# Hybrid decoder block on one core: the opening's hand-written order carried on to the fourth product of the first seven-product block

## The chip, the core and the metric

One core of a Trainium2 chip runs the whole program: TensorE (PE in the profile) multiplies, VectorE (DVE) and ScalarE (ACT) prepare operands and post-process, GpSimd (POOL) fills a few constants, SyncE (SP) issues the large transfers. PEld are TensorE's weight loads. The metric is the device time of one execution in microseconds (us). The kernel before takes 1735.16 us, the median of 3 runs (1734.92 to 1735.41).

## What is computed

A macaron block: a SwiGLU feed-forward part, a token mixer, a second feed-forward part, and a norm. The change touches the start of the first feed-forward part, and the place where the mixer's small vectors are loaded.

```python
D_MODEL, SEQ, D_FF, FFN_RESIDUAL_SCALE = 2048, 256, 5632, 0.5

def rms_norm(x, gain):
    var = jnp.mean(x * x, axis=-1, keepdims=True)
    return x * lax.rsqrt(var + NORM_EPS) * gain

def swiglu_ffn(x, w_gate, w_up, w_down):
    return (jax.nn.silu(x @ w_gate) * (x @ w_up)) @ w_down

x = x + FFN_RESIDUAL_SCALE * swiglu_ffn(rms_norm(x, ffn1_norm), w_gate, w_up, w_down)
...
z = rms_norm(x, mix_norm) @ w_in
```

Everything is float32. x has 256 rows of 2048 columns, the gate and up matrices have 2048 x 5632 elements.

## The kernel before

**Products in three parts.** A float32 operand is split into a high part (a cast to a shorter format, called `hi`, made by ScalarE) and a low part (`lo`, the rest, made by VectorE as a difference). A product is then hi x hi, lo x hi and hi x lo, accumulated in one bank of the accumulator memory. Weights come in units of 512 rows by 512 columns: four slices of 128 rows. One unit of weights against one half of x (128 rows) is 12 matrix instructions of 128x512: 8 with the weights' high part, 4 with their low part; against both halves it is 24 (`multiply`, lines 211 to 226). A unit is loaded as `raw`, 1 MB. `parts_of` (line 197) makes `hi` in two casts of 128x1024 and `lo` in one instruction of 128x2048. High and low parts live in two rotating buffers and, for every third unit, in a third one (`split_tiles`, line 183), so a new unit's cast waits until the product that used its buffer is done.

**The first 512 columns of gate and up** are made by `begin` (line 569), whose order is written out by hand and kept on every engine, since `Engine.pinned` is set (lines 36 to 44, 671). x has four parts of 512 columns, called units 0 to 3. Units 0 and 1 are transposed unnormalised (`turn`, with the gain applied), since the norm's factor is only known when all of x has been squared; the banks are scaled by the factor afterwards (`scale_banks`). Units 2 and 3 are normalised first and then transposed (`scaled`, `turn_scaled`). `squares` sums the squares on ScalarE, `factor` and `diagonals` make the factor, `rows` spreads it by two small products. `plain` keeps the sum of the transposed high and low parts for units 0 and 1, which `scale` and `split` later turn into normalised operands. Before the data arrive, `keep_busy` issues dummy products on a bank that nobody reads; they keep TensorE working.

**The seven-product blocks.** All further columns of gate and up go through `seven` (line 377) in pairs of 512 columns. For units 0 and 1 of x and two columns of weights it is a two-by-two block product with seven products instead of eight, with sums of weights (`w12 - w11`, `w22 - w11`, `w22 - w12`, `w21 - w11`, on VectorE, in place) and sums of x (`seven_of`: `spare`, `two`, `last`, with `high` and `low` for their split). Units 2 and 3 of x take part as ordinary products (`usual`). TensorE's work in the block, in program order:

- `product_of(0)`, `product_of(4)`: 12 instructions each; in the profile `ps_g_a` and `ps_g_c`, with weights `hi_g_p`, `lo_g_p`
- `usual(0, b2)`: 24, into `ps_g_e` and `ps_g_c`, with `hi_g_x`, `lo_g_x`
- `product_of(5)`: 12; `usual(1, b3)`: 24; `product_of(6)`: 12; `product_of(2)`: 12
- `usual(0, a2)`: 24; `product_of(3)`: 12; `usual(1, a3)`: 24; `product_of(1)`: 12

The results `a` and `c` of some products are copied out by ScalarE (`snap`: `s1`, `s5`, `u2`, `u3`), since the bank is used again or the value is needed twice. `between` is called at fixed places with a number or a name and lets the caller put other work there. In the kernel before, `meanwhile` (line 773) drops the pinning at the first of these places, after the second product; from there a list scheduler orders every engine's work but SyncE's, by its own model of the times. After the third product it makes the remaining sums of x (`sums`), after the fourth the hidden tiles of the first 512 columns (`first_hidden`: silu of gate times up).

**Queues.** The large loads are issued by SyncE in the order of the program. GpSimd issues ten small loads of vectors for the mixer at the very start (`load_vectors`, lines 116 and 138 to 161): two groups, `many` and `conv`, which `prepare` (line 801) transposes much later, in the middle of the first feed-forward part.

In `begin` the loop over the four slices of unit 0 stands like this:

```python
for j in range(UK):
    norm.turn((j,))
    high(0, "g", quarters[j : j + 1])
    low(0, "g", quarters[j : j + 1])
    if j:
        products(j - 1)
products(UK - 1)
```

Of the kernel before, what the change touches and what calls it, by code (L numbers as in the profile page):

```python
# [49 lines left out]
def hybrid_block(ctx: ExitStack, tc: tile.TileContext, a: dict, out: bass.AP):  # L50
# [53 lines left out]
    act.activation(early, ones[:, :1], AF.Copy, scale=1.0)  # L104
# [11 lines left out]
    def load_vectors(group, name, engine):  # L116
# [19 lines left out]
    keep_busy(2)  # L136
    pe.held = False
    turns = [
        load_vectors(
            [  # L140
                ("mix_norm", a["mix_norm"][0], 16),
                ("ffn2_norm", a["ffn2_norm"][0], 16),
                ("lru_lambda", a["lru_lambda"][0], 8),
                ("lru_conv_b", a["lru_conv_b"][0], 8),
                ("lru_b_a", a["lru_b_a"][0].rearrange("h d -> (h d)"), 8),
                ("lru_b_i", a["lru_b_i"][0].rearrange("h d -> (h d)"), 8),
                ("lru_out_norm", a["lru_out_norm"][0], 8),
                ("sc_out_norm", a["sc_out_norm"][0], 8),
            ],
            "many",  # L150
            nc.gpsimd,
        ),
        load_vectors(
            [
                ("lru_conv_w", a["lru_conv_w"][0].rearrange("k d -> (k d)"), 32),
                ("sc_conv_w", a["sc_conv_w"][0].rearrange("k d -> (k d)"), 24),
            ],
            "conv",
            nc.gpsimd,
        ),  # L160
    ]
# [49 lines left out]
    def multiply(targets, blk, apart=False, middle=None, late=None):  # L211
# [4 lines left out]
        for ps, st, begin, _ in targets:  # L216
            for j in range(UK):
                pe.matmul(ps, st[j][0], blk[j][0], start=begin and j == 0, stop=False, **more)
                pe.matmul(ps, st[j][1], blk[j][0], start=False, stop=False, **more)
# [9 lines left out]
    class Norm:  # L229
# [5 lines left out]
        def squares(self, c):  # L235
            for t in range(NT):
# [109 lines left out]
    def seven_of(sf, x0, x1, v, spare, parts):  # L346
# [25 lines left out]
        high(4)  # L372
        low(4)
# [5 lines left out]
    def seven(w, rows, cols, sf, xs, name, keep, done, between=None):  # L379
# [23 lines left out]
        def usual(i, raw, n, *targets):  # L403

            blk = parts_of(raw, f"{name}_x{i}{n}")
# [36 lines left out]
    def ffn(tag, norm, after, opening=False):  # L442
        with tc.tile_pool(name=f"ffn{tag}", bufs=1, side="left") as fp:
# [89 lines left out]
            def sums():  # L533

                if not left:
                    pair = [big(f"xs{tag}_{i}") for i in range(2)]
                    halves = [(b[:, :, o : o + P], b[:, :, o + P : o + S]) for b in pair for o in (0, S)]
                    left.append(seven_of(sf, units[0], units[1], vs, quad(keep(f"spare{tag}")), halves))
# [26 lines left out]
            def joint(u, m, blk, middle=None, late=None):  # L565
                x = norm.xT[u] if u < 2 else units[u]
                multiply([(ps[m, t], stationary(x, t), u == 0, u % 2 == 1) for t in range(NT)], blk, True, middle, late)

            def begin():
# [17 lines left out]
                def mm(u, m, middle=None, late=None):  # L587
                    joint(u, m, blocks(*parts[u, m]), middle, late)
# [14 lines left out]
                for j in range(UK):  # L603
# [38 lines left out]
                mm(1, "u", norm.rows, lambda: turn_both(2))  # L642
# [21 lines left out]
                sums()  # L664
                low(3, "u")
# [17 lines left out]
            def first_hidden():  # L683
                for t in range(NT):
# [3 lines left out]
                    waiting.append((0, t, sg, False))  # L688

# [60 lines left out]
            for s in range(5):  # L750
# [22 lines left out]
                def meanwhile(i):  # L773
                    if i == "sum":
                        return
# [359 lines left out]
```

## Time and profile before

| | us |
|---|---|
| median of 3 runs | 1735.16 |
| the profiled execution, its own time | 1735.13 |
| its span, from the first to the last instruction | 1733.4 |
| TensorE busy in the span | 1722.0 |
| VectorE busy | 1478.2 |
| ScalarE busy | 1047.3 |
| GpSimd busy | 6.9 |

The granted TensorE clock over the span is 0.999 of full speed. A row of the timeline has the start, the duration, the engine, the line, the operation, what it writes and reads with shapes, and the number of instructions merged into it; in brackets how long the engine stood idle before, and what it waited for. Nearly all instructions carry line 43, that of the wrapper `Engine`, so the tile names tell them apart: `ps` are accumulator banks, `pt` and `ph` transposes, `raw` loaded weights, `xres` is x, `xT` and `x` its transposed operands, `xs` the operands made of sums, `junk` the squares. A trailing letter or number of a buffer is left out of the names.

In rows by stretches of time, each engine's busy time and number of instructions are followed by the granted clock, the busy share of the transfer engines, and the GB/s they moved.

### The profile page before, as it was taken

How to read it: one execution, taken by the hardware profiler on the slowest of the kernel's cores; microseconds unless marked ns; L12 is line 12 of the kernel's file. 1: busy time of each engine (PE TensorE's matmuls, PEld its weight loads, DVE VectorE, ACT ScalarE, POOL GpSimd, SP SyncE). 2: the span in 40 equal slices, each digit the busy share in tenths (PEclk: the TensorE clock that was granted, in tenths of full speed). 3: DMA queues.
4: the chain of work that ended last, by engine and by line, in shares of the span. 5: the costliest groups of instructions: out<-in, count | busy, mean ns of one | idle time of the engine just before them, and what ended most of it. 6: DMA issues, size and time to landing. Idle time of an engine off the chain costs nothing.

```text
span 1733.4 us, 20352 instructions
## 1 busy us (share of the span) xinstructions
PE 1722.0 (99%) x8045; PEld 1439.9 (83%) x8045; DVE 1478.2 (85%) x1213; ACT 1047.3 (60%) x1354; POOL 6.9 (0%) x32
## 2 busy tenths in 40 slices
PE   9999999999999999999999999999999999999998
PEld 8788888888888888888888888888888888888886
DVE  7998989889789898687986668889899888899895
ACT  7666565656466666565655446656556664556654
POOL 1000000000000000000000000000000000000000
PEclk9999999999999999999999999999999999999999
DMA  7664665566466556555555764565665646555743
GB/s 275 213 219 146 217 221 192 199 238 218 151 205 210 201 180 218 172 170 193 177 189 183 247 209 137 194 243 177 215 214 194 215 149 218 194 194 195 255 157 122
DMA packets 174224, 343.24 MB, mean 198 GB/s; under 512 B 5684, under 2 KB 8624, under 8 KB 174000
## 3 DMA queue, kind: packets, MB, share of 16 engines
q1 hardware_dynamic: 173632, 340.81, 57.5%
q8 instruction: 63, 1.03, 0.2%
q10 hardware_dynamic: 176, 1.06, 0.2%
q14 instruction: 33, 0.27, 0.0%
q0 software_dynamic: 320, 0.07, 0.0%
HBM read 339.82 MB, written 2.10 MB: 197 GB/s over the span
## 4 chain that ended last, share of the span: by engine, by line
PE 97%; DVE 2%; issue 0%; DMA 0%; ACT 0%; DVEq 0%
PE ps_d L43 13%; PE ps_in L43 13%; PE ps_u_a L43 9%; PE ps_g_a L43 9%; PE ps_u_c L43 6%; PE ps_g_c L43 6%; PE ps_d_a L43 5%; PE ps_o L43 5%; PE ps_u_d L43 5%; PE ps_g_d L43 5%; PE ps_d_c L43 3%; PE ps_u_e L43 3%; PE ps_g_e L43 3%; PE ps_g L43 3%; PE ps_u L43 3%; PE ps_d_d L43 3%
## 5 line engine op out<-in xcount | busy, mean ns | idle before, releaser
L43 ACT CAST hi_g_p<-raw_g 128x1024 fp32r<-128x1024 f32 x140 | 142.5, 1050 | 103.1 <-DVE raw_g L43 28.3
L43 DVE TENSOR_TENSOR lo_g_p<-raw_g,hi_g_p 128x2048 fp32r<-128x2048 f32 x70 | 159.5, 2287 | 33.3 <-ACT hi_g_p L43 33.1
L43 ACT CAST hi_u_p<-raw_u 128x1024 fp32r<-128x1024 f32 x140 | 141.3, 1049 | 68.4 <-PE ps_u_a L43 22.9
L43 DVE TENSOR_TENSOR lo_u_p<-raw_u,hi_u_p 128x2048 fp32r<-128x2048 f32 x70 | 159.2, 2287 | 20.6 <-ACT hi_u_p L43 20.2
L43 PE MATMUL ps_d<-hi_d,h 128*128 128x512 f32 x704 | 168.0, 390 | 0.0
L43 PEld LDWEIGHTS ps_d<-hi_d,h 128*128 128x128 f32 x704 | 131.5, 188 | 26.9
L43 PE MATMUL ps_in<-xT_nm,hi_in 128*128 128x512 f32 x640 | 153.4, 391 | 0.1
L43 PEld LDWEIGHTS ps_in<-xT_nm,hi_in 128*128 128x128 f32 x640 | 117.4, 188 | 23.5 <-DVE bc_nm L43 0.6
L43 ACT CAST hi_d<-raw_d 128x1024 fp32r<-128x1024 f32 x88 | 88.6, 1047 | 70.0 <-PE ps_u_d L43 22.4
L43 DVE TENSOR_TENSOR lo_d<-raw_d,hi_d 128x2048 fp32r<-128x2048 f32 x44 | 100.6, 2290 | 30.5 <-ACT hi_d L43 30.5
L43 DVE TENSOR_TENSOR lo_in<-raw_in,hi_in 128x2048 fp32r<-128x2048 f32 x40 | 91.4, 2286 | 39.4 <-ACT hi_in L43 35.5
L43 ACT CAST hi_in<-raw_in 128x1024 fp32r<-128x1024 f32 x80 | 80.0, 1045 | 67.2 <-PE ps_in L43 46.0
L43 ACT CAST hi_d_p<-raw_d 128x1024 fp32r<-128x1024 f32 x84 | 85.0, 1049 | 58.8 <-DVE raw_d L43 40.0
L43 ACT CAST hi_g_x<-raw_g 128x1024 fp32r<-128x1024 f32 x80 | 81.4, 1048 | 42.2 <-PE ps_g_c L43 24.6
L43 ACT CAST hi_u_x<-raw_u 128x1024 fp32r<-128x1024 f32 x80 | 80.5, 1047 | 36.5 <-PE ps_u_c L43 19.6
L43 DVE TENSOR_TENSOR lo_d_p<-raw_d,hi_d_p 128x2048 fp32r<-128x2048 f32 x42 | 95.6, 2287 | 7.8 <-ACT hi_d_p L43 7.7
L43 DVE TENSOR_TENSOR raw_u<-raw_u,raw_u 128x2048 f32<-128x2048 f32 x40 | 91.6, 2290 | 9.3 <-DMA raw_u<-in_ffn_w_up_dram 8.6
L43 DVE TENSOR_TENSOR lo_g_x<-raw_g,hi_g_x 128x2048 fp32r<-128x2048 f32 x40 | 91.5, 2286 | 6.6 <-ACT hi_g_x L43 6.6
L43 DVE TENSOR_TENSOR raw_g<-raw_g,raw_g 128x2048 f32<-128x2048 f32 x40 | 91.5, 2289 | 3.4 <-DMA raw_g<-in_ffn_w_gate_dram 2.9
L43 DVE TENSOR_TENSOR lo_u_x<-raw_u,hi_u_x 128x2048 fp32r<-128x2048 f32 x40 | 91.4, 2286 | 2.1 <-ACT hi_u_x L43 1.9
L43 PE MATMUL ps_d<-lo_d,h 128*128 128x512 f32 x352 | 87.3, 389 | 0.0
L43 PEld LDWEIGHTS ps_in<-xT_nm,lo_in 128*128 128x128 f32 x640 | 82.1, 191 | 3.1
(363 smaller groups left out, 3568.7 us busy)
## 6 DMA issues: line engine op xcount, KB each, us to landing
raw_d<-in_ffn_w_down_dram SPq DMA_DIRECT2D x88, 1024.0 KB, 5.1
raw_u<-in_ffn_w_up_dram SPq DMA_DIRECT2D x87, 1024.0 KB, 5.1
raw_g<-in_ffn_w_gate_dram SPq DMA_DIRECT2D x86, 1024.0 KB, 5.1
raw_in<-in_w_in_dram SPq DMA_DIRECT2D x40, 1024.0 KB, 5.0
raw_o<-in_w_out_dram SPq DMA_DIRECT2D x16, 1024.0 KB, 5.1
xres<-in_x_dram SPq DMA_DIRECT2D x3, 512.0 KB, 10.2
raw_g<-in_ffn_w_gate_dram SPq DMA_DIRECT2D x4, 256.0 KB, 5.1
raw_u<-in_ffn_w_up_dram SPq DMA_DIRECT2D x2, 512.0 KB, 8.7
```

The lines of the kernel that those rows point to most:

```text
L43: ins = getattr(self.engine, name)(*args, **kwargs)
```

## The change

1. The first activation, which loads ScalarE's function table, is a square root instead of a copy, so the table with the square root is loaded at the start and not at the norm's factor.
2. The two dummy products between the transposition of the first gain vector and the first transposes of x are gone. One is issued ahead of the first products instead, and the last two slices of unit 0 are transposed before the second slice's products.
3. The transfers of the second half of up's unit 0 and of gate's unit 1 are issued earlier than x's second and third quarters, respectively.
4. Squares, casts and low parts from unit 0 of up to unit 1 of up are cut into halves and interleaved in another order. `multiply` takes `pieces`: the products with high parts go over both halves of x for the first two slices, then for the last two. `within` places the transposes of unit 1 inside up's unit 0.
5. `low(3, "u")` stands between the cast and the low part of the first sum of x.
6. In the first block of gate (`early`) the pinning holds until the fourth product of sums is done (`product_of(6)`). The sums of x are made at named places: `two` after `w12 - w11`; the casts and low parts of two operands behind the second product; `last` with its cast and low part after `w22 - w12`. `w22 - w11` and the parts of `b2` are made earlier, with one cast of 128x2048. `first_hidden` follows the copy `u3`.
7. The mixer's vectors are loaded after `first_hidden`: `load_vectors` first copies a column of the second hidden tile into the row tile on GpSimd, so its loads wait for that tile.

The core of the diff:

```diff
-    act.activation(early, ones[:, :1], AF.Copy, scale=1.0)
+    act.activation(early, ones[:, :1], AF.Sqrt)
...
-    def load_vectors(group, name, engine):
+    def load_vectors(group, name, engine, after=None):
...
+        if after is not None:
+            engine.tensor_copy(rows[:, :1], after[:n, :1])
...
     first_turn()
-    keep_busy(2)
     pe.held = False
-    turns = [
-        load_vectors(
...
+    turns = []
+    def load_more(after):
+        turns.extend(
...
-    def multiply(targets, blk, apart=False, middle=None, late=None):
+    def multiply(targets, blk, apart=False, middle=None, late=None, pieces=(range(UK),), within=None):
...
+        for js in pieces:
+            for i, (ps, st, begin, _) in enumerate(targets):
+                if within and js is pieces[-1] and i == len(targets) - 1:
+                    within()
+                for j in js:
...
         dve.tensor_tensor(spare, a21, a22, op=ALU.add)
         high(4)
+        if meanwhile:
+            meanwhile()
         low(4)
...
         product_of(0, w11, a, True)
         dve.tensor_tensor(w11, w12, w11, op=ALU.subtract)
+        if early:
+            between("first sum")
         product_of(4, w11, c, True)
-        s1 = snap(a, "s1")
+        blk = None
+        if early:
+            between("second product")
+            hi, lo = split_tiles(f"{name}_x01")
+            act.copy(hi, b2)
+            s1 = snap(a, "s1")
+            dve.tensor_tensor(w11, w22, w11, op=ALU.subtract)
+            low_part(b2, hi, lo)
+            blk = blocks(hi, lo)
+        else:
+            s1 = snap(a, "s1")
         s5 = snap(c, "s5")
...
-        usual(0, b2, 1, (e, 1, True, not two), (c, 0, False, False))
+        usual(0, b2, 1, (e, 1, True, not two), (c, 0, False, False), first=blk)
...
-        dve.tensor_tensor(w11, w22, w11, op=ALU.subtract)
+        if not early:
+            dve.tensor_tensor(w11, w22, w11, op=ALU.subtract)
...
         dve.tensor_tensor(w12, w22, w12, op=ALU.subtract)
+        if early:
+            between("third sum")
         product_of(6, w12, a)
         u3 = snap(a, "u3")
+        if early:
+            between("fifth product")
...
-                    if j:
-                        products(j - 1)
-                products(UK - 1)
-
-                fetch(0, "u", ends, lambda i: load_x(1) if i == 0 else None)
+                    if j == 1:
+                        keep_busy(1)
+                        products(0)
+                for j in range(1, UK):
+                    products(j)
+
+                fetch(0, "u", ends)
+                load_x(1)
+                fetch(1, "g", ends)
                 load_x(2)
-                fetch(1, "g", ends)
                 load_x(3)
-                high(0, "u")
-                his, los = turn(1)
-                his()
-                norm.squares(0)
-                low(0, "u", ends)
-                los()
+                js = (range(2), range(2, UK))
+                high(0, "u", ends[:1])
+                norm.squares(0, (0,))
+                low(0, "u", ends[:1])
+                high(0, "u", ends[1:])
+                norm.squares(0, (1,))
+                low(0, "u", ends[1:])
+
+                def second():
+                    his, los = turn(1)
+                    his()
+                    los()
+
+                mm(0, "u", None, None, js, second)
+
+                high(1, "g")
                 plain(0)
-                mm(0, "u")
-
-                high(1, "g")
+                low(1, "g", ends)
+                plain(1)
                 norm.squares(1)
                 norm.squares(2)
-                low(1, "g", ends)
-                plain(1)
-                mm(1, "g")
+                mm(1, "g", None, None, js)
 
                 fetch(1, "u")
                 fetch(2, "g")
-                high(1, "u")
-                norm.squares(3)
-                low(1, "u")
+                norm.squares(3, (0,))
+                high(1, "u", ends[:1])
+                norm.squares(3, (1,))
+                low(1, "u", ends[:1])
+                high(1, "u", ends[1:])
                 norm.factor()
                 norm.diagonals()
+                low(1, "u", ends[1:])
...
-                sums()
-                low(3, "u")
+                sums(lambda: low(3, "u"))
...
+                if opening:
+                    load_more(sg)
...
                     if opening and s == 0:
-                        Engine.pinned = False
-                        if i:
-                            (sums, first_hidden)[i - 1]()
+                        two, last, high, low = left[0]
+                        if i == "first sum":
+                            two()
+                        elif i == "second product":
+                            for k in (5, 6):
+                                high(k)
+                                low(k)
+                        elif i == "third sum":
+                            last()
+                            high(2)
+                            low(2)
+                        elif i == "fifth product":
+                            Engine.pinned = False
+                            first_hidden()
...
-                seven(wg, (0, 1), cs, sf, xs, f"g{tag}_{s}", keep, gate, meanwhile)
+                seven(wg, (0, 1), cs, sf, xs, f"g{tag}_{s}", keep, gate, meanwhile, opening and s == 0)
```

More of the change, by code (lines that the diff above doesn't have):

```diff
@@ L209, in stationary @@
         return [(tile[:, j, t * P : (t + 1) * P], tile[:, j, S + t * P : S + (t + 1) * P]) for j in range(UK)]
-    def multiply(targets, blk, apart=False, middle=None, late=None):
+    def multiply(targets, blk, apart=False, middle=None, late=None, pieces=(range(UK),), within=None):
         more = dict(skip_group_check=True) if apart else {}
[L216 to L219, printed above, removed]
+        for js in pieces:
[3 more added lines that the diff above has]
+                for j in js:
+                    pe.matmul(ps, st[j][0], blk[j][0], start=begin and j == 0, stop=False, **more)
+                    pe.matmul(ps, st[j][1], blk[j][0], start=False, stop=False, **more)
         if middle:
@@ L233, in __init__, with squares @@
             self.ss = work.tile([P, NT, NC_D], F32, tag="ss", name=f"ss_{name}")
-        def squares(self, c):
-            for t in range(NT):
+        def squares(self, c, ts=range(NT)):
+            for t in ts:
                 junk = work.tile([P, CW], F32, tag="junk", name=f"junk_{self.name}_{c}_{t}", bufs=1)
@@ L341, in product, with seven_of @@
         return ps
-    def seven_of(sf, x0, x1, v, spare, parts):
+    def seven_of(sf, x0, x1, v, spare, parts, meanwhile=None):
         a11, a12, a21, a22 = v[0, 0], v[0, 1], v[1, 0], v[1, 1]
@@ L377, in quad, with seven @@
         return tile.rearrange("p (j c) -> p j c", j=UK)
-    def seven(w, rows, cols, sf, xs, name, keep, done, between=None):
+    def seven(w, rows, cols, sf, xs, name, keep, done, between=None, early=False):
         a, c, e, d = (bank(f"ps_{name}_{n}") for n in "aced")
@@ L531, in normalise, with sums @@
                 split(u)
-            def sums():
+            def sums(meanwhile=None):
                 if not left:
@@ L537, in sums @@
                     halves = [(b[:, :, o : o + P], b[:, :, o + P : o + S]) for b in pair for o in (0, S)]
-                    left.append(seven_of(sf, units[0], units[1], vs, quad(keep(f"spare{tag}")), halves))
+                    spare = quad(keep(f"spare{tag}"))
+                    left.append(seven_of(sf, units[0], units[1], vs, spare, halves, meanwhile))
                 else:
@@ L585, in low, with mm @@
                         low_part(*(z[:, i:e, :] for z in [raw[u, m]] + parts[u, m]))
-                def mm(u, m, middle=None, late=None):
-                    joint(u, m, blocks(*parts[u, m]), middle, late)
+                def mm(u, m, *more):
+                    joint(u, m, blocks(*parts[u, m]), *more)
                 def turn(c):
```

59 lines of the change are left out of this document (31 added, 28 removed).

## The prediction, made before the changed kernel was run

> **What bounds the kernel now.** I read the page's totals and its chain first, then the list of waits, then the chain in order of time.
>
> ```profile
> span 1733.4 us, 20352 instructions
> PE 1722.0 (99%) x8045; PEld 1439.9 (83%) x8045; DVE 1478.2 (85%) x1213; ACT 1047.3 (60%) x1354; POOL 6.9 (0%) x32
> ...
> PE 97%; DVE 2%; issue 0%; DMA 0%; ACT 0%; DVEq 0%
> ```
>
> TensorE is busy for 99% of the span and makes 97% of the chain that ended last. Only where it stands still, or runs slowly, is there anything to win. The list of its waits, over the whole run, has three entries:
>
> ```profile
> PE idle L43 <- DVE ones L43: 1.1, 1, 1.1
> PE ps_g_e L43 <- DVE lo_g_x L43: 0.8, 1, 0.8
> PE ps_g L43 <- ACT hi_g L43: 0.6, 1, 0.6
> ```
>
> All three lie in the part that the diff rewrites. The chain in order of time shows how much is lost there (start, duration, work, number of instructions):
>
> ```profile
> 3.83 1.15 PE idle L43 x4
> 4.98 0.44 PE pt_n L43 x2
> ...
> 5.44 0.47 ACT xT_n L43
> 5.92 0.52 ACT hi_g L43
> ...
> 6.48 2.93 PE ps_g L43 x6
> ...
> 9.82 1.38 PE ps_g L43 x6
> ...
> 14.20 0.87 PE pt_n L43 x8
> ...
> 49.98 5.45 PE ps_u L43 x24
> ...
> 97.52 2.72 PE ps_u_a L43 x12
> ```
>
> 24 products in 5.45 us are 0.227 us each; eight transposes in 0.87 us are 0.109 each. From the first transpose (4.98) to 14.20 stand 24 products and 8 transposes, 6.3 us of work in 9.22: 2.9 lost. From 14.20 to the first product of the block (49.98 + 5.45 = 55.43) nearly nothing is lost. The block's 180 products (15 groups of 12) need 40.9 us and take 97.52 - 55.43 = 42.1: 1.2 lost. With the 4.98 before the first transpose, that is about 9 us; nothing else can be won here. The sum is made against this execution's 1735.13 us (span 1733.4 and 1.7 around it), 0.03 below the median of the runs.
>
> **The opening.** Two dummy products stand ahead of the first transposes: the filler runs to 4.98, and the transposes follow at once. Had their data landed by then? Issue to landing, four transfers issued at 0.74, 1.23, 2.20 and 2.68:
>
> ```profile
> xres<-in_x_dram SPq DMA_DIRECT2D x1, 256.0 KB, 3.2
> raw_g<-in_ffn_w_gate_dram SPq DMA_DIRECT2D x1, 256.0 KB, 3.3
> xres<-in_x_dram SPq DMA_DIRECT2D x1, 256.0 KB, 6.4
> raw_g<-in_ffn_w_gate_dram SPq DMA_DIRECT2D x1, 256.0 KB, 6.5
> ```
>
> The first x piece is there at 3.94, so without that filler the transposes start near 4.05, 0.93 earlier. The copy of the transposed x (0.47) and the cast of the weights (0.52; landed at 4.53) follow them, so the first product starts at about 5.55 instead of 6.48. The one dummy that is left, now ahead of it, runs in the gap of that wait (two passes of 1.15/4 = 0.29 us, to about 5.5) and costs nothing.
>
> Those first products are slow:
>
> ```profile
> 6.48 2.08 PE L43 MATMUL ps_g<-hi_g,xT_n 128*128 128x512 f32 x4 [0.64 <-ACT hi_g L43]
> 9.48 1.27 PE L43 MATMUL ps_g<-hi_g,xT_n 128*128 128x512 f32 x4
> ```
>
> Four take 2.08 us, later 1.27, and two transposes 0.44 at first against 0.22 later: TensorE runs at half rate until about 9.4. After the change six slow products end at 5.55 + 2.93 = 8.48, then come both pairs of transposes that are left (before, one pair). They need the second x piece, which landed at 8.6; they end at 9.05 (full rate) to 9.5 (half rate). The other 18 products, 4.09 us, end at 13.1 to 13.6, against 14.20. Whether that piece lands earlier is the question of the vector loads, now gone from here:
>
> ```profile
> 5.50:6.00 0.50, 0.33 (x2) 0.00 (x0) 0.05 (x1) 0.50 (x2) 0.50 (x2) 1.00 1.22 220
> 9.00:9.50 0.50, 0.50 (x4) 0.30 (x3) 0.00 (x0) 0.00 (x0) 0.00 (x0) 1.00 1.08 402
> ```
>
> The queues moved 220 GB/s (last column) while GpSimd was issuing them, 402 right after. An earlier landing wins 0.1 us at most, since the slow products end at 8.48 anyway. I take 1.0 us of gain; bounds: 0 (piece and clock both late) and 2.7 (full rate from 5.9 on: the six products end near 7.0, then 0.44 and 4.09 to 11.5).
>
> **Between the opening and the block** TensorE has no idle time to give, so the edits only have to stay hidden. The split casts, sums of squares and root on ScalarE are reordered. From the first transpose of unit 1 (time 0) TensorE reaches unit 1 of up after 8 transposes, 12 products left of up's unit 0 and 24 of gate's unit 1, 9.0 us later. ScalarE does four copies, two casts, five squares and one cast by then:
>
> ```profile
> 15.13 1.56 ACT L43 ACTIVATE xT_n<-pt_n,cols_first 128x256 fp32r<-128x256 f32 x4
> 25.38 0.63 ACT L43 ACTIVATE junk_n<-xres 128x512 f32<-128x512 f32 x1
> 25.92 0.19 ACT L43 ACTIVATION_READ_ACCUMULATOR junk_n<-xres 128x1 f32 x1
> 26.12 1.28 ACT L43 ACT_TABLE_LOAD   x1
> 55.07 2.01 ACT L43 CAST hi_g_p<-raw_g 128x1024 fp32r<-128x1024 f32 x2 [1.66 <-DVE raw_g L43]
> ```
>
> 0.3 + 1.56 + 2.0 + 5 x 0.75 + 1.0 = 8.6: 0.4 to spare. The second cast (8.6 + 0.8 + 1.0 = 10.4) is wanted at 10.8. The table load that goes (1.28) lay on ScalarE alone, under TensorE's products, and wins nothing by itself. The swapped transfers move up's second half and gate's unit 1 forward and x's third quarter back by two 512 KB pieces (2.6 us at the 402 GB/s above); its squares have that time. So I cost all of this at nothing; without that cover it would be half a microsecond.
>
> **The block.** Here the fixed order now reaches on, and the order that the built program has for ScalarE decides. Times here are on the axis of the profile above, its first product at 55.43; P0, P4, P5, P6, P2 are the products of sums, X2 and X3 the ordinary ones on units 2 and 3.
>
> ```
> hi P4 x2 | hi xs x2 | hi X2 | copy s1 | copy s5 | hi P5 x2 | hi P2 (1st half) | copy u2 | hi X3 x2 |
> hi P2 (2nd half) | hi xs | hi P6 x2
> ```
>
> Durations, each row its kind (low parts and sums on VectorE follow each other by 2.20 us, small ones by 0.60, as the starts 49.87, 52.07, 52.67 show):
>
> ```profile
> 43.48 2.29 DVE L43 TENSOR_TENSOR lo_g<-raw_g,hi_g 128x2048 fp32r<-128x2048 f32 x1
> ...
> 49.87 2.28 DVE L43 TENSOR_TENSOR lo_g_p<-raw_g,hi_g_p 128x2048 fp32r<-128x2048 f32 x1
> 52.07 0.68 DVE L43 TENSOR_TENSOR v<-spare,v 128x512 f32<-128x512 f32 x1
> 52.67 2.29 DVE L43 TENSOR_TENSOR raw_g<-raw_g,raw_g 128x2048 f32<-128x2048 f32 x1
> ...
> 58.88 0.57 ACT L43 COPY s_g<-ps_g_a 128x512 f32<-128x512 f32 x1
> ...
> 63.43 0.73 PE L43 MATMUL ps_g_e<-lo_g_x,x 128*128 128x512 f32 x2 [0.75 <-DVE lo_g_x L43]
> ```
>
> - Old wait removed. VectorE from 43.48: low of gate unit 3, spare, low of up unit 3 (46.3), xs, low P0 (49.1), w12-w11 (51.3 to 53.6), two sums to 54.8; hi P4 53.6 to 55.6; low P4 to 57.9; two xs lows, w22-w11 59.0 to 61.3, low X2 61.2 to 63.5. TensorE does P0, P4, X2 back to back and wants that last low part at 55.43 + 5.45 + 3.63 = 64.5. So the 0.75 goes, with the rest of the 1.2.
> - First new wait. P5 runs 66.3 to 69.0. X3 follows it, but its casts stand on ScalarE behind the copy u2 of P5's result: half of hi P2 (needs P5's high products, 68.1 to 69.2), u2 0.57, first half of hi X3 1.0, to 70.7. TensorE stands 1.7 us, and behind it everything of the block.
> - Second. hi X3 ends at 71.7; VectorE, idle till then, does low X3 to 74.0, w22-w12 to 76.2, the last xs sum to 76.8; ScalarE its cast (0.64) to 77.5 and hi P6's first half to 78.5. X3 ends at 70.7 + 5.45 = 76.2; one product of P2 fits at 77.5, P6 starts at 78.5: 2.0 us lost.
>
> P6 and P2 then end at 83.7 (the 24 products of both, from 76.2, and 2.0). The 72 products behind them need 16.3 us and find their parts ready. ScalarE, from P6's end at 82.8: copy u3 to 83.4, the table load of 1.28, and four of these,
>
> ```profile
> 75.16 1.09 ACT L43 ACTIVATE sg<-ps_g 128x512 f32<-128x512 f32 x2
> ```
>
> to 86.9; then hi of the last X (first half 87.9, wanted at 89.1) and hi P3, behind its sum (87.0 to 89.2), to 91.2. VectorE: low of that X to 91.4, low P3 to 93.6, wanted at 94.1. The block ends at 100.0 instead of 97.5. Lost in it: 3.7 instead of 1.2, so +2.5. Bounds: +1.7 (the second wait half covered) to +3.3 (the half cast and both waits a little longer).
>
> **The vector loads later.** GpSimd's two copies wait for the second hidden tile (VectorE, 87.0), then ten transfers are issued; the mixer turns them hundreds of microseconds later. Their neighbours are transfers like these:
>
> ```profile
> raw_u<-in_ffn_w_up_dram SPq DMA_DIRECT2D x1, 1024.0 KB, 5.1
> ...
> rows_many<-in_lru_lambda_dram POOLq DMA_DIRECT2D x1, 4.0 KB, 5.5
> ```
>
> The second up block wants w12, which is now issued when low P3 is done (93.6) and lands at 98.7; w12-w11 ends at 101.1, its first cast at 102.1, and TensorE wants it at 100.0 + 2.72 = 102.7. That is 0.6 to spare, so nothing in the sum.
>
> Sum: -1.0 + 2.5 = +1.5 us: 1736.6. Nothing behind changes its order on TensorE, and no wait is listed there.
>
> **Rivals.**
> 1. The clock is let go early. The dummy now closes a gap of 0.64 us in TensorE's work, so full rate from about 5.9: gain 2.7, sum -0.2, 1734.9. For it: nearly unbroken work from 1.05 on. Against: before, the engine also worked from 1.05 to 5.8 and was still slow at 6.48. [...]
> 2. Slower: the vector loads hold up w12. Two x pieces of one size took 3.2 us and, among the vector loads, 6.4. If w12 is held by the same 3.2 it lands at 101.9, its sum ends at 104.2, the cast at 105.2: TensorE stands 2.5 us, sum +4.0, 1739.1. It decides from a landing later than 99.3. For it: 220 GB/s above. Against: at 93 us few other transfers are queued. [...]
> 3. The block gains as meant: no new wait shows, -1.0 - 1.2, 1732.9. It would need X3's cast to start before P5's end, against the order above.
> 4. The opening wins nothing (the second x piece and the clock as late as the old order had them): 1737.6.
>
> **Chances.** Forecast 0.54 (own range 1735.8 to 1737.5), early clock 0.15, vector loads 0.14, block as meant 0.07, no gain in the opening 0.10. The range 1733.3 to 1739.2 holds all but the ends of rivals 2 and 3. About 0.2% (3.5 us) is what a measurement of this kernel can tell from no change: below 1731.7 only rival 3 with an early clock, 0.04; above 1738.6 nearly all of rival 2 and a late clock beside rival 4, 0.17; within, 0.79.
>
> **What would show it.** In the profile after: the first product near 5.5; the first wait gone at lo_g_x; two new entries among TensorE's waits, for ScalarE's casts hi_g_x (1.7) and hi_g_p (about 2.0 with the xs cast); VectorE idle for several microseconds near 67; the second block's first product 1.5 us later than 97.5. I am wrong if X3 starts right behind P5, if the first products run at full rate from the start, or if TensorE waits in the second block.

## The result, and the profile after

| | us |
|---|---|
| median of 22 runs, changed kernel | 1737.57 (1735.62 to 1739.70) |
| median of 22 runs, kernel before | 1735.18 (1733.40 to 1735.94) |
| ratio, 95% interval | 1.0018 (1.0011 to 1.0024) |
| the profiled execution, its own time | 1738.35 |
| its span | 1736.3 |

The changed kernel is 2.4 us slower, 0.14%. The list of TensorE's waits over the whole run of the changed kernel (what waited, for what; total, times, longest) now has eight entries:

```profile
PE ps_g_e L43 <- ACT hi_g_x L43: 1.7, 1, 1.7
PE idle L43 <- DVE ones L43: 1.1, 1, 1.1
PE ps_g_c L43 <- ACT xs L43: 1.0, 1, 1.0
PE ps_d_a L43 <- DVE lo_d_p L43: 0.9, 1, 0.9
PE ps_g_a L43 <- ACT hi_g_p L43: 0.4, 1, 0.4
PE ps_u_c L43 <- ACT hi_u_p L43: 0.3, 1, 0.3
PE ps_g L43 <- ACT hi_g L43: 0.2, 1, 0.2
PE pt_n L43 <- DMA xres<-in_x_dram: 0.2, 1, 0.2
```

The old wait of 0.75 for `lo_g_x` is gone. Three new ones stand in the block (1.7, 1.0, 0.4), a small one at the first transposes (0.2), one in the up block (0.3), and one that the prediction didn't look for stands in the last down stage (0.9). Four marks place the loss; the first three are starts of timeline rows in both profiles:

| start of | before | after | difference | stage |
|---|---|---|---|---|
| first product of the block | 55.26 | 54.02 | -1.24 | opening: -1.24 |
| first product of the up block | 97.36 | 98.83 | +1.47 | block: +2.71 |
| first down product | 139.96 | 142.01 | +2.05 | up block: +0.58 |
| end of the span | 1733.4 | 1736.3 | +2.9 | all the rest: +0.85 |

The opening, in TensorE's timeline of the changed kernel (start, duration, work, number, and in brackets the idle time ahead of it):

```profile
3.99 1.11 PE L43 MATMUL pt_n<-ident,xres 128*128 128x128 f32 x4 [0.18 <-DMA xres<-in_x_dram]
...
5.75 2.08 PE L43 MATMUL ps_g<-hi_g,xT_n 128*128 128x512 f32 x4 [0.22 <-ACT hi_g L43]
7.62 0.77 PE L43 MATMUL ps_g<-lo_g,xT_n 128*128 128x512 f32 x2
8.23 0.60 PE L43 MATMUL pt_n<-ident,xres 128*128 128x128 f32 x4
8.58 1.17 PE L43 MATMUL ps_g<-hi_g,xT_n 128*128 128x512 f32 x4
```

Two low products take 1.05 us at half rate and 0.62 later. Here they take 0.77, so the rate changed under them. Each trace also holds records of the granted clock, and the first of them gives the moment from which it was full: 7.92 us after the span's start here, 9.69 in the kernel before. (The rows by stretches of time can't show this moment: they count the clock as full wherever no record says otherwise, and give 1.00 for the opening too.) The start is 0.73 earlier than before (5.75 against 6.48). So more than that start went into the 1.24 of this execution; the experiments show how the two share it.

The block, on TensorE, ScalarE and VectorE of the changed kernel:

```profile
66.71 1.07 PE L43 MATMUL ps_g_a<-lo_g_p,xs 128*128 128x512 f32 x4
69.44 2.14 PE L43 MATMUL ps_g_e<-hi_g_x,x 128*128 128x512 f32 x8 [1.66 <-ACT hi_g_x L43]
...
74.14 1.07 PE L43 MATMUL ps_g_c<-lo_g_x,x 128*128 128x512 f32 x4
76.17 0.50 PE L43 MATMUL ps_g_c<-hi_g_p,xs 128*128 128x512 f32 x1 [0.95 <-ACT xs L43]
77.12 2.15 PE L43 MATMUL ps_g_a<-hi_g_p,xs 128*128 128x512 f32 x8 [0.45 <-ACT hi_g_p L43]
```

```profile
66.91 1.05 ACT L43 CAST hi_g_p<-raw_g 128x1024 fp32r<-128x1024 f32 x1 [4.52 <-PE ps_g_a L43]
67.86 0.58 ACT L43 COPY u_g<-ps_g_a 128x512 f32<-128x512 f32 x1
68.34 1.99 ACT L43 CAST hi_g_x<-raw_g 128x1024 fp32r<-128x1024 f32 x2
...
75.50 0.62 ACT L43 CAST xs<-v 128x512 fp32r<-128x512 f32 x1 [4.21 <-DVE v L43]
```

```profile
70.37 2.29 DVE L43 TENSOR_TENSOR lo_g_x<-raw_g,hi_g_x 128x2048 fp32r<-128x2048 f32 x1 [5.65 <-ACT hi_g_x L43]
72.58 2.29 DVE L43 TENSOR_TENSOR raw_g<-raw_g,raw_g 128x2048 f32<-128x2048 f32 x1
74.78 0.69 DVE L43 TENSOR_TENSOR v<-v,v 128x512 f32<-128x512 f32 x1
```

ScalarE has nothing to do for 4.52 us, then makes half of hi P2, the copy u2 and only then hi X3. VectorE waits 5.65 us for that cast, and everything it does next (low X3, `w22 - w12`, the last sum) is late by as much. That is the order that the prediction read out of the program. Counted from start to start, with 0.227 for each product, the first gap is 1.8 us (66.71 + 0.91 to 69.44) and the second 1.8 too (74.14 + 0.91 to 77.12, less one product); the idle time in brackets is smaller, since a row's end is modelled. With somewhat slower products behind each gap (behind the first, 2.14 us for eight against 1.98 in x3_ahead, below) the block takes 4.0 us more than the 40.8 that x3_ahead needs for the same work.

In the last down stage VectorE scales the final norm's gain (`fin`) as soon as it has landed. The row of the kernel before, and then the rows of the changed one:

```profile
1651.77 0.43 DVE L43 TENSOR_SCALAR fin<-fin 128x512 f32<-128x512 f32 x1 [1.88 <-DMA fin<-in_final_norm_dram]
```

```profile
1654.71 0.43 DVE L43 TENSOR_SCALAR fin<-fin 128x512 f32<-128x512 f32 x1 [3.04 <-DMA fin<-in_final_norm_dram]
...
1675.35 2.29 DVE L43 TENSOR_TENSOR lo_d_p<-raw_d,hi_d_p 128x2048 fp32r<-128x2048 f32 x1 [0.86 <-ACT hi_d_p L43]
1677.70 1.19 PE L43 MATMUL ps_d_a<-lo_d_p,hs 128*128 128x512 f32 x4 [0.88 <-DVE lo_d_p L43]
```

The transfer landed 7.5 us after its issue instead of 6.3. VectorE stood 3.0 us for it instead of 1.9, and twenty microseconds later TensorE stood 0.88 for a low part that VectorE made late.

### The profile page after: what moved, and what is told of

Its sections match the earlier page's. It is cut to its first block, busy times and chain, and to the rows that moved or that the text cites. A ratio compares the mean times of both kernels' runs of the same rounds, so it can differ in the third digit from the quotient of the medians.

```text
span 1736.3 us, 20346 instructions
## 1 busy us (share of the span) xinstructions
PE 1721.9 (99%) x8043; PEld 1439.0 (83%) x8043; DVE 1477.6 (85%) x1214; ACT 1045.1 (60%) x1352; POOL 11.3 (1%) x34
## 4 chain that ended last, share of the span: by engine, by line
PE 92%; DVE 1%; DMA 0%; ACT 0%; issue 0%; DVEq 0%
PE ps_d L43 13%; PE ps_in L43 13%; PE ps_u_a L43 9%; PE ps_g_a L43 8%; PE ps_u_c L43 6%; PE ps_g_c L43 6%; PE ps_d_a L43 5%; PE ps_o L43 5%; PE ps_u_d L43 5%; PE ps_g_d L43 4%; PE ps_u_e L43 3%; PE ps_d_c L43 3%; PE ps_g_e L43 3%; PE ps_d_d L43 3%; PE ps_d_e L43 1%; PE ps_g L43 1%
## 5 line engine op out<-in xcount | busy, mean ns | idle before, releaser
L43 ACT CAST hi_g_x<-raw_g 128x1024 fp32r<-128x1024 f32 (+1 forms) x79 | 81.4, 1058 | 41.7 <-PE ps_g_c L43 24.8
```

Source lines behind the costliest of these rows:

```text
L43: ins = getattr(self.engine, name)(*args, **kwargs)
```

## The experiments

Twelve kernels follow; the kernel before ran beside each (medians 1734.96 to 1735.26). Each is the median of 10 or 11 runs whose times lie 2 to 4.5 us apart. The difference of two such medians is uncertain by about one microsecond, so what is smaller is read from the profiles or not at all.

**X3's split ahead of u2 (x3_ahead).**

```diff
-        product_of(5, w11, a)
...
+            five, blk = parts_of(w11, f"{name}_p5"), parts_of(b3, f"{name}_x11")
+            multiply([(a, sf[5], False, True)], five, True)
...
         u2 = snap(a, "u2")
```

> The changed kernel, but the split of X3's weights (two casts on ScalarE, the low part on VectorE) is issued ahead of the copy u2 of P5's result instead of behind it. Theory (the block's two new waits come from that place on ScalarE): hi X3 is made near 62.5 to 64.5 us, its low part by 67, w22-w12 and the last sum by 70; the 1.7 us at hi_g_x goes, and with it the 1.4 us at xs and hi_g_p, because VectorE no longer stands still from 64.7 to 70.4. 3.1 us less than the changed kernel's 1737.6: about 1734.5. Rival 1 (only the first wait hangs on that place, the sums are late by themselves): 1.7 less, 1735.9, with the xs wait still in the list. Rival 2 (the up block is tied to the landing of its w12, so what is won ahead of it is waited away there): the wait at hi_u_p grows from 0.3 to about 3, time 1737 or more.

1733.51 us, 4.1 below the changed kernel, where 3.1 were expected. From its timelines:

```profile
61.40 2.00 ACT L43 CAST hi_g_x<-raw_g 128x1024 fp32r<-128x1024 f32 x2
...
65.81 1.07 PE L43 MATMUL ps_g_a<-lo_g_p,xs 128*128 128x512 f32 x4
66.72 1.98 PE L43 MATMUL ps_g_e<-hi_g_x,x 128*128 128x512 f32 x8
68.53 1.98 PE L43 MATMUL ps_g_c<-hi_g_x,x 128*128 128x512 f32 x8
```

hi X3 starts 8.3 us after the block's first product instead of 14.3, X3 follows P5 at once, and all three waits of the block are gone with one move. The block takes 40.8 us (53.12 to 93.92), which is its work, against 44.8 in the changed kernel. The expectation had added up only the listed idle time. Both waits hung on that place; rivals 1 and 2 fall.

**The sums ahead of u2, X3's casts left (sum_ahead).**

```diff
         product_of(5, w11, a)
+        if early:
+            dve.tensor_tensor(w12, w22, w12, op=ALU.subtract)
+            between("third sum")
         u2 = snap(a, "u2")
...
```

> The changed kernel, but the third sum (w22-w12), the last sum of the x quarters, its cast and the parts of P6 and P2 are issued ahead of the copy u2, into VectorE's idle time; X3's casts stay behind u2. Theory (two waits, each with its own cause): the waits at xs and hi_g_p (1.4 together) go; the one at hi_g_x stays, and grows from 1.7 to about 2.1 because one more cast stands ahead of u2: 1.0 less than the changed kernel, about 1736.6. Rival (the second wait is only a consequence of the first): nothing changes, 1737.6.

1737.69 us: no gain, and yet the waits at xs and hi_g_p are off the list. TensorE's timeline shows what took their place:

```profile
70.97 3.59 PE L43 MATMUL ps_g_e<-hi_g_x,x 128*128 128x512 f32 x8 [2.18 <-ACT hi_g_x L43]
74.36 2.14 PE L43 MATMUL ps_g_c<-hi_g_x,x 128*128 128x512 f32 x8
```

The first wait grew from 1.66 to 2.18 as expected, but the eight products behind it took 3.59 us instead of 2.14. Either the clock had fallen back or the weights' second half came late. The same trace decides it, in rows by stretches of time (the granted clock stands third from the end):

```profile
70.00:71.00 1.00, 0.03 (x1) 0.03 (x1) 0.22 (x1) 1.00 (x2) 0.00 (x0) 1.00 0.00 0
71.00:72.00 1.00, 1.00 (x3) 0.79 (x4) 0.10 (x1) 1.00 (x2) 0.00 (x0) 0.61 0.00 0
...
73.00:74.00 1.00, 1.00 (x4) 0.72 (x3) 1.00 (x1) 1.00 (x2) 0.00 (x0) 0.50 0.00 0
74.00:75.00 1.00, 1.00 (x5) 0.82 (x4) 1.00 (x2) 0.71 (x1) 0.00 (x0) 0.68 0.00 0
75.00:76.00 1.00, 1.00 (x6) 0.82 (x5) 1.00 (x1) 0.00 (x0) 0.00 (x0) 1.00 0.54 96
```

By its records the clock was at half from 71.22 to 74.63, for 3.41 us, and at full for the 61.44 us before that. TensorE had stood the 2.18 us up to 70.97, which is 0.25 ahead of 71.22.

**Dummy products in that gap (sum_fill, after_fill).** Seven in sum_ahead, five in the changed kernel, both in the first block alone:

```diff
...
+            for _ in range(7):
+                pe.matmul(d[:, :P], ones, ones, start=True, stop=True, skip_group_check=True)
         if two:
             usual(1, b3, 1, (e, 1, False, True), (c, 0, False, False))
```

> sum_ahead, with seven dummy products of 128 columns issued on TensorE between P5 and X3, into the bank ps_g_d, which is started anew later. In sum_ahead TensorE stood 2.18 us there, and X3's first eight products then took 3.59 us instead of 1.98. Theory (a wait of that length lets the clock fall back to half rate): seven dummies (about 1.8 us) keep TensorE at work, X3 starts no earlier, its first eight products take 2.0 to 2.2, and the time is up to 1.6 less than sum_ahead's 1737.7: about 1736.2. Rival (those eight products were slow because the second half of their weights came late, since hi X3 is made in two casts): they take 3.6 again, 1737.7.

TensorE's timeline of sum_fill at that place:

```profile
68.76 1.72 PE L43 MATMUL ps_g_d<-ones 128*128 128x128 f32 x14
71.11 2.14 PE L43 MATMUL ps_g_e<-hi_g_x,x 128*128 128x512 f32 x8 [0.62 <-ACT hi_g_x L43]
```

1735.98 us, 1.7 below sum_ahead, by work that computes nothing. X3 starts no earlier after P5's last product, but its eight products take 2.14 again, and the granted clock stays at 1.00 there. So the 2.18 us of standing had let the clock fall back, and the products behind paid 1.5 us in the profiled execution; how many others it strikes is not shown. Without it the block takes 43.3 us (55.16 to 98.50) against the changed kernel's 44.8: sum_ahead's edit is worth 1.5, the second wait less the 0.5 by which the first has grown. The medians say 1.6.

> The changed kernel, with five such dummies (about 1.3 us) between P5 and X3, where it stands 1.66 us. In the one profile of the changed kernel the eight products after that wait ran at full rate (2.14 us), but its times reach from 1735.6 to 1739.7. Theory (in some executions the clock falls back there, in others not): the upper times go, median 0.4 to 0.8 less than 1737.6. Rival (1.66 us is too short for it, the spread comes from elsewhere): the same median and spread, 1737.6.

1738.31 us against 1737.57: nothing won. 1.66 us of standing did not do it here: the changed kernel's trace has no record of a lower clock in the block. The rival holds, and the wide spread of the changed kernel is not shown to come from there.

**The old block behind the new opening (old_block), and the reverse (old_opening).** The first puts back the old `meanwhile` and the old place of `low(3, "u")` behind the sums, and calls `seven` without `early`:

```diff
-                seven(wg, (0, 1), cs, sf, xs, f"g{tag}_{s}", keep, gate, meanwhile, opening and s == 0)
+                seven(wg, (0, 1), cs, sf, xs, f"g{tag}_{s}", keep, gate, meanwhile)
```

> The changed kernel's opening, its order up to the block and its later vector loads (here in the same place, behind the first hidden tiles), with the block of the kernel before (sums, casts and copies placed as there). Theory (opening gains, block loses): the block starts 1.2 us earlier than in the kernel before and takes its old 42.1 us: 1734.0 against 1735.2 before. Rival (the gain of the opening is eaten by the old block's wait at lo_g_x, which ends with VectorE's chain and not with TensorE): the wait grows from 0.75 to 2, 1735.2. Rival 2 (the vector loads cost it): 1735.5 or more, with a wait at the first casts of the up block.

1735.44 us, 0.3 above the kernel before where 1.2 below was expected. The block kept its 42.1 us (54.97 to 97.04) and its wait at lo_g_x its 0.75: rival 1 falls, as does the wait in the up block. What failed is the opening, which won 0.29 in this execution, and 0.87 was lost at lo_d_p in the last down stage.

The second puts the old order of `begin` up to the fetch of up's third unit and the two dummies back:

```diff
+    keep_busy(2)
...
-                js = (range(2), range(2, UK))
-                high(0, "u", ends[:1])
...
+                high(0, "u")
+                his, los = turn(1)
...
```

> The opening of the kernel before (its filler, its order of casts, squares and transfers up to the third unit) with the changed kernel's block and its later vector loads. Theory (in most executions the new opening is worth 0.3, the rest of the changed kernel's 2.4 is the block and what follows it): 2.1 to 2.4 over before plus that 0.3: about 1737.8. Rival (the opening is worth the 1.2 that the changed kernel's profile shows): 1738.8.

1737.54 us, 2.6 over the kernel before beside it and the same as the changed kernel (1737.57). The block makes the whole loss by itself, and the new opening shows no worth in the median. The rival's 1.2 lies at the edge of what two such medians leave open.

**The dummies put back, all else as changed (filler).**

```diff
     first_turn()
+    keep_busy(2)
     pe.held = False
```

> The changed kernel with the two dummy products ahead of the first transposes put back (the one ahead of the first product stays). The first transposes come about 0.8 us later. Theory (products run at half rate until the clock is let go at a moment that they don't set, so a start that is later by T costs T/2): block start = 47.3 + half of the sum of the first product's start and the moment of release, 0.4 later than in the changed kernel with the same release: about 1738.0. Rival (a later start costs all of it): 0.8 more, 1738.4. Rival 2 (the dummies bring the release forward): 1737.5 or less.

1738.52 us, 0.95 above the changed kernel, nearer to the rival's 0.8 than to the theory's 0.4, but the medians can't separate the two. The profiles can, since each trace records from when the clock was full (the last column). While it is at half, products take twice as long (in the kernel before four take 1.87 us from start to start at 6.48 and 0.93 at 12.65), so half of the time between the first product and that moment should be lost. In thirteen of the profiles the block start less half of the sum of the two is 47.1 to 47.3 us, and in x3_ahead, whose clock was full before the first product, the way from there to the block is 53.12 - 5.81 = 47.3 too:

| | first product | block start | clock full from |
|---|---|---|---|
| old opening: before | 6.48 | 55.26 | 9.69 |
| before_vec_late | 6.42 | 55.70 | 10.67 |
| before_fin | 6.45 | 55.85 | 10.98 |
| old_opening | 6.42 | 55.98 | 11.20 |
| new opening: changed | 5.75 | 54.02 | 7.92 |
| x3_ahead | 5.81 | 53.12 | 4.72 |
| x3_fin | 5.75 | 53.82 | 7.42 |
| old_block_fin | 5.72 | 54.60 | 9.09 |
| old_block | 5.89 | 54.97 | 9.83 |
| sum_ahead | 6.03 | 55.03 | 9.78 |
| vec_early | 6.07 | 55.14 | 9.95 |
| sum_fill | 6.10 | 55.16 | 9.86 |
| after_fill | 5.68 | 55.25 | 10.56 |
| filler (dummies back) | 6.42 | 54.30 | 7.59 |

With the clock full from 9.7 to 9.8, an earlier first product by 0.45 (sum_ahead) or 0.59 (old_block) brought the block forward by 0.23 and 0.29: about one half. So 0.37 of the changed kernel's 1.24 comes from its earlier start, and the rest from its earlier clock (half of 9.69 - 7.92). That moment moves over 6.5 us between the profiled executions, and from the first product on it is worth up to 2.7 us of block start. It was 9.7 to 11.2 in the four with the old opening and 4.7 to 10.6 in the ten with the new one; whether the new opening brings it forward is not shown by so few. The extremes, in TensorE's timelines: four products at full rate at 5.81 in x3_ahead, and still four at half rate at 9.43 in old_opening:

```profile
5.81 1.21 PE L43 MATMUL ps_g<-hi_g,xT_n 128*128 128x512 f32 x4 [0.57 <-ACT hi_g L43]
```

```profile
9.43 1.98 PE L43 MATMUL ps_g<-hi_g,xT_n 128*128 128x512 f32 x4
```

**The vector loads (vec_early, before_vec_late).** In vec_early they are issued at the start again:

```diff
+    load_more()
+
     def big(name):
...
-                if opening:
-                    load_more(sg)
```

> The changed kernel, but the mixer's vector loads are issued from GpSimd at the start, as in the kernel before. Theory (the loads' place is worth nothing either way): the second x piece lands up to 0.4 us later (8.6), at most 0.3 of it is seen by TensorE; the first casts of the up block no longer wait (0.25 to 0.4 less): 1737.6, within 0.4. Rival (vector loads late hold up w12 and what follows): 0.6 to 1 less, 1736.8. Rival 2 (vector loads early hold up the opening): the first transposes or products come later by over 0.5, 1738.2.

1737.92 us, 0.35 above the changed kernel. The first casts of the up block did not stop waiting. They waited longer, with no vector load near them, as the timelines of VectorE and TensorE show:

```profile
100.94 2.29 DVE L43 TENSOR_TENSOR raw_u<-raw_u,raw_u 128x2048 f32<-128x2048 f32 x1 [3.13 <-DMA raw_u<-in_ffn_w_up_dram]
104.37 1.20 PE L43 MATMUL ps_u_c<-hi_u_p,xs 128*128 128x512 f32 x4 [1.53 <-ACT hi_u_p L43]
```

The changed kernel has 98.53 and 0.25 there. The transfers of w12, of vec_early and then of the changed kernel (KB, us from issue to landing):

```profile
raw_u<-in_ffn_w_up_dram SPq DMA_DIRECT2D x1, 1024.0 KB, 7.4
```

```profile
raw_u<-in_ffn_w_up_dram SPq DMA_DIRECT2D x1, 1024.0 KB, 6.1
```

So what holds up w12 is its own transfer. The lone piece that the prediction took as its price needed 5.1; here other 1 MB pieces are issued some two microseconds before and after it, and three in such a row in the kernel before took 6.6 to 6.9. That the company is the cause fits these rows, but no run took the neighbours away.

Nor were the vector loads the reason why x's second piece took 6.4 us in the opening of the kernel before: it took 5.0 in vec_early, with them, and 6.2 in filler, without.

before_vec_late moves the loads alone, in the kernel before, with the `load_more` of the diff.

> The kernel before, with its opening and block as they were, and only the mixer's vector loads moved to where the changed kernel has them. Theory A (the loads' place does nothing): 1735.2, within 0.3; what the profile of the last down stage shows at the final norm's gain (its landing 6.3 us after its issue, no wait of TensorE) is chance. Theory B (the four profiles with late vector loads all have TensorE waiting 0.6 to 0.9 us at lo_d_p, the two with early ones don't): the gain lands 6.8 to 7.5 us after its issue and TensorE waits there, 0.6 to 0.9 more: 1735.9. Theory C (the 32 KB less among the first transfers help the opening): the second x piece lands earlier, 0.3 less.

1734.90 us against 1735.26 beside it: theory A, 0.3 below its 1735.2; C would give the same. The gain landed after 6.4 us and TensorE waited 0.2, so B falls: late vector loads by themselves don't make the gain late.

**The instruction on the final gain (x3_fin, before_fin, old_block_fin).** All three drop it:

```diff
-                    dve.tensor_scalar(lastgain, lastgain, -0.5, None, op0=ALU.mult)
...
+        half = single("fh")
+        dve.tensor_scalar(half, r, -0.5, None, op0=ALU.mult)
...
-                dve.scalar_tensor_tensor(xo, xo, r, fin[:, o], op0=ALU.mult, op1=ALU.mult)
+                dve.scalar_tensor_tensor(xo, xo, half, fin[:, o], op0=ALU.mult, op1=ALU.mult)
```

> x3_ahead, and the small VectorE instruction that scales the final norm's gain by -0.5 as soon as it has landed is left out; the factor is put into the row scale at the end (one instruction on 128x1 more for each half of the rows). In x3_ahead VectorE stood 2.4 us for that landing, and TensorE 0.6 us behind it. Theory (that instruction passes a transfer's lateness on to VectorE's queue): no wait at lo_d_p, 0.4 to 0.6 less than x3_ahead's 1733.5: 1733.0. Rival (the first use of the gain, some 12 us later, or the two instructions more at the end take it back): 1733.5 or more.

1732.49 us, 1.0 below x3_ahead (of which the wait at lo_d_p was 0.6 in the profile), ratio to the kernel before 0.9986 (0.9978 to 0.9995): faster than both kernels. TensorE's list of waits holds nothing any more behind the opening:

```profile
PE idle L43 <- DVE ones L43: 1.1, 1, 1.1
PE ps_g L43 <- ACT hi_g L43: 0.2, 1, 0.2
PE pt_n L43 <- DMA xres<-in_x_dram: 0.2, 1, 0.2
```

> The kernel before, with the small instruction on the final norm's gain left out and its factor put into the row scale, as in x3_fin. Theory (VectorE passes the lateness of that transfer on in some executions of every kernel): in those executions of the kernel before where the gain lands late TensorE waits too, so the median falls by 0.3 to 0.8, to about 1734.7. Rival (in the kernel before the wait of 1.9 us stays inside VectorE's slack): 1735.2.

1734.90 us against 1734.96 beside it: the rival. In the kernel before VectorE's slack holds that wait.

> old_block (new opening, block of the kernel before), with the instruction on the final norm's gain left out as in x3_fin and before_fin. Against before_fin only the opening, the edits hidden behind it and the place of the vector loads differ. Theory (the opening is worth 0.3, and old_block gave that back at the late gain): 0.3 less than before_fin's 1734.9, 0.8 less than old_block's 1735.4: 1734.6. Rival 1 (the opening is worth its full 1.0 once that wait is out): 1733.9. Rival 2 (the wait at the gain was no loss of the median): 1735.4.

1734.36 us: 1.1 below old_block and 0.5 below before_fin. Nearest to the theory's 1734.6, but 0.5 is less than these medians can tell from nothing. What they do show is the late gain: TensorE's wait at lo_d_p, 0.87 in old_block, is off the list, though the gain landed 6.8 us after its issue. That the opening wins a little, and that the changed kernel and old_block give it back at the gain, fits the numbers and is not shown by them.

Why the gain lands later behind the new opening stays open. Of the eight profiles with the new opening and that instruction seven show TensorE waiting at lo_d_p (0.4 to 0.9), with the gain landing 6.6 to 7.5 us after its issue; the eighth (vec_early) 6.1 us and no wait. The three with the old opening show 5.9 to 6.4 us and 0.2 at most. No run changed the neighbours of that transfer.

## Why the prediction was right, and where it was off

The forecast was 1736.6 with a range to 1739.2; measured 1737.57, just above the likeliest case's own range (1737.5), and within 0.2% of no change, as held most likely. Its sum was -1.0 + 2.5. The profiled execution has -1.24 + 2.71, and 1.4 more in two places that were costed at nothing. The 0.9 of its opening that came from the clock was luck: without it this execution would have been near 1739.2, the end of the range.

- **Old wait removed:** right. It is off the list.
- **First new wait, 1.7:** right in place, cause and size (1.66 listed, 1.8 from start to start). x3_ahead shows the cause.
- **Second new wait, 2.0:** right in place, cause and size: 1.8 from start to start, and a little more for the slower products behind it. sum_fill won 1.5 by removing it, with the first wait grown by 0.5. The order, half of hi P2, u2, hi X3, low X3, `w22 - w12`, last sum, xs cast, stands in the rows as it was read from the program. The block lost 3.9 us against its 40.9 of work, forecast 3.7.
- **Opening, gain 1.0:** the mechanism was right (the transposes start as their data land, 3.99 against 4.05 forecast), the term was mis-sized. Two steps of it failed. The first product starts at 5.7 to 6.1, not 5.55, 1.76 us after the first transpose and not the 1.5 that I took. And I let the slow products end earlier by all of the earlier start, where full rate need not come earlier with it: half of it counts. With the same clock moment in both, the gain is 0.2 to 0.4.
- **Rival 1, an early clock:** it is not one case but a moment that differs between the profiled executions. The changed kernel's profile has some of it (7.92), x3_ahead's all of it (4.72). That closing the gap of 0.64 us would bring full rate from 5.9 on, from which its 2.7 is worked out, was the author's estimate, and no run shows it: with the gap down to 0.22 us in nine profiles, the clock became full at 7.42 to 10.56. TensorE worked nearly without a break from 1.05 in all fourteen, and ten of them have 9.1 to 11.2. What sets the moment was not shown.
- **Rival 4 (the opening wins nothing, 1737.6)** was given 0.10, and the median is its time. By old_opening its account isn't refuted either: the new opening showed no worth in the median. Its reason holds in part, since the clock came nearly as late in most profiles (9.1 to 10.6 in six of the nine others with that opening), while x's second piece held up nothing: in the changed kernel it landed at 6.7 and its transposes came at 8.23.
- **Hidden edits from 14 to 55 us, costed at nothing:** right. No wait of TensorE stands there in the changed kernel.
- **Vector loads later, costed at nothing, and rival 2:** right in sum, with the wrong reason for the margin. The 0.6 to spare went, because w12's transfer took 6.1 and not the 5.1 taken from a lone one. The vector loads are not needed for it: vec_early waits more without them, in its one profile. The up block lost 0.58.
- **Not foreseen:** the late gain in the last down stage, 0.9 in the profile. I had written that nothing behind changes; the order doesn't, the landing did.
- **Rival 3 (no new wait, 1732.9)** is what one more move gives: x3_ahead, 1733.5.

## What to carry to other kernels

When a hand-written order is carried on, list for each engine what stands between a cast and the instruction that its own inputs really wait for: here one copy of a product's result, and half of another cast, in front of one that could have run six microseconds earlier, cost both waits. Work that is pulled ahead while TensorE runs at half rate counts half (0.45 and 0.59 us of earlier start brought 0.23 and 0.29). An instruction placed on a busy engine only because its transfer should have landed ties the whole queue to that transfer: here VectorE stood 3.0 us for it, and TensorE 0.88 for a low part behind it.

## What the runs showed of the hardware

- Standing for 2.18 us in a stream of products at full rate was followed by 3.41 us of half the granted clock, in which eight products took 3.59 us instead of 2.14; filling the gap with dummies took that away. Gaps of 1.53 and 1.66 us had no such sequel in any profile here: behind 1.66 the eight products took 2.14 us each time (changed kernel, filler, old_opening, vec_early), behind 1.53 four took 1.20 (vec_early). In sum_ahead the clock went to half 0.25 us after the standing ended; what lies between 1.66 and 2.18 was not measured.
- By the traces' records the clock became full between 4.72 and 11.20 us in fourteen executions that all begin with the same five dummies near 1.05. Of a start that comes earlier while it is at half, half is won (0.23 of 0.45 in sum_ahead, 0.29 of 0.59 in old_block). The 2.7 us that the moment can be worth are about as wide as the times of the kernel before lie apart (1733.4 to 1735.9); that it is the cause is not shown.
